# Encoder layer on one core: the second group's queries, keys and values as block products in a stage of their own

## The chip, the cores and the metric

The kernel runs on one core of a Trainium2 chip, in one launch. The metric is the device time of that core in microseconds, from the start of the program to its end. Lower is better. Each kernel is timed in several executions, and one more execution is recorded by the profiler.

## The reference

One layer (DEPTH is 1) over 2048 frames of width 1024, with 16 heads of 64 and an FFN of width 2816, all in fp32. Chunk c of 64 frames attends to itself and to the 8 chunks before it, with a learned relative bias for each head.

```
def rms_norm(x, g):
    return x * rsqrt(mean(x * x, axis=-1) + 1e-6) * g

# each chunk c of 64 frames, k0 = max(0, (c - 8) * 64), k1 = (c + 1) * 64
sc = einsum('bhqd,bhkd->bhqk', q[chunk c], k[:, :, k0:k1]) * 64 ** -0.5 + bias
o  = einsum('bhqk,bhkd->bhqd', softmax(sc), v[:, :, k0:k1])

h = rms_norm(x, g_pre_mix);  q, k, v = split_heads(h @ w_qkv)
x = x + rms_norm(merge_heads(o) @ w_o, g_post_mix)
h = rms_norm(x, g_pre_ffn)
x = x + rms_norm((silu(h @ w_gate) * (h @ w_up)) @ w_down, g_post_ffn)
```

## The kernel before

**Tiles.** The 2048 frames are two groups (NG) of 1024, each of two halves of 512 (HALF). Features lie on the 128 partitions, in eight blocks of 128 (KT), and frames run along the columns. An fp32 product is made of three matmuls over values that are split into a high and a low part: high by high, high by low, low by high (`products`, L187 to L191). Weights come from DRAM as raw tiles and are split on ScalarE and VectorE (`split_part`, L124).

**Stages.** First the attention of group 0 with its queries, keys and values, then that of group 1 with its own, then the FFN of both groups (`gate_up`, `down`). The FFN's products are already done by seven block products in place of eight (`Blocks`; the names B11, B21, T1, T2, B22, T3, T4 are the seven column sides, and `FACTOR` gives the weight block or sum of blocks of each). The weight sums S1 to S4 are made in DRAM by SyncE copies and by accumulating copies that GpSimd issues (`weight_sums`), one step at a time during the attention.

**Attention.** `Attend` is one half of one pair of heads: 16 jobs in a group, each of four query blocks of 128 frames. For one query block, TensorE makes the scores of both heads (tile `st`, L549 and L550), VectorE adds the bias and takes the maximum (L558), ScalarE takes the exponential and its sum (L562), VectorE the reciprocal (L565), GpSimd scales (L566). Then TensorE transposes (tile `tt`, L582 for four key blocks, L593 for the fifth), and ScalarE and VectorE copy the result to SBUF as `pT` (L585, L587, L594). The weighted sum of the values (`output`, tile `po`, L611) comes once in four query blocks, for the whole job.

**What fills in.** The dense products of queries, keys (`qk_job`), values (`v_job`) and of w_o (`o_half`) are a generator, `dense`, that yields after each product. `fill` takes products from it between the attention's parts, at the rate that the due times ask for; `until` takes them until a named result is there. Each product gives one credit to a list of small steps (`later`, `tick`): norms, loads, splits, each with a price. `drain` runs all that is left in the list at once. In group 0's `o_half` the small steps load and norm group 1's input (`Prep`) and end the first half (`Post.write`: y times its row scale times the gain, plus the residual, stored as `x1_d`). In the FFN the class `Late` does the like for y that was put into DRAM (`sums`, `rstd`, `write`; L1136 and L1139).

**Order.** TensorE's order is the order of the program, written out by hand (`manual_schedule` for PE). The order on the other engines and on SyncE's DMA queue is set by a scheduler. Results of `o_half` for group 0 stay in SBUF. `y`, `res` and the columns that are loaded share one ring of three buffers of 128x512 (tag `io`).

```
def tick(w):
    credit[0] += w
    while later and credit[0] >= later[0][0]:
        cost, step = later.popleft()
        credit[0] -= cost
        step()

def drain():
    while later:
        later.popleft()[1]()
```

## Time and profile before

| what | value |
|---|---|
| three timed runs | 2445.75, 2446.17, 2447.52 us (median 2446.17) |
| profiled execution | 2441.23 us |
| span of its trace | 2439.5 us |
| mean granted TensorE clock | 0.995 |
| TensorE busy (matmul) | 2400.2 us, 98% |
| VectorE, ScalarE, GpSimd busy | 60%, 42%, 12% |
| group 0's last weighted sum | ends near 485 us |
| group 1's attention | to about 1056 us |
| first FFN matmul | 1149 us |
| DMA | 488.41 MB, 200 GB/s on average |

The busy share is an average over the stages. Where TensorE is full, a stage is as long as its matmuls. What ended an idle stretch of an engine is named behind an arrow in the profile's rows (`<-`). An instruction's duration there is longer than its distance to the next one, since matmuls are pipelined: the price of a matmul is the distance of two starts.

### The profile page before, as it was taken

Reading aid. Unit: us, or ns where it says so; the run is one execution under the profiler, and the core shown is the slowest. Engines: PE = TensorE matmul, PEld = TensorE weight load, DVE = VectorE, ACT = ScalarE, POOL = GpSimd, SP = SyncE. Lnnn points to the kernel's source line nnn. Section 1 sums busy time; section 2 is a strip of 40 time slices with the busy share of each in tenths; the row PEclk is TensorE's granted clock in tenths of the full one; section 3 lists DMA queues with packets and bytes.
Section 4 is the critical chain, followed back from the end, with each engine's and each line's share of the span. In section 5 each row is a group of like instructions: output and inputs, shape, how many; then the busy total and the mean of one; then the engine's idle time right before and its main releaser. Section 6 shows DMA issues by size and latency. Waiting matters only on the chain.

```text
span 2439.5 us, 34920 instructions
## 1 busy us (share of the span) xinstructions
PE 2400.2 (98%) x12554; PEld 1994.3 (82%) x12554; DVE 1466.2 (60%) x2569; ACT 1033.1 (42%) x1807; POOL 299.2 (12%) x379
## 2 busy tenths in 40 slices
PE   9999999899999999999999999999999999999997
PEld 8887887688888888778888788888888888888886
DVE  6555454577455554567567665577566655555577
ACT  5444444554344443455333333365343333334444
POOL 0223333202232322310000000000000000000001
PEclk9999999999999999999999999999999999999999
DMA  7689999957777766646476755477667655457654
GB/s 223 179 213 245 257 263 230 271 185 211 197 192 189 181 157 144 163 146 229 152 260 206 244 174 167 123 247 256 208 211 250 219 178 160 136 169 243 196 187 147
DMA packets 209884, 488.41 MB, mean 200 GB/s; under 512 B 25360, under 2 KB 27424, under 8 KB 208432
## 3 DMA queue, kind: packets, MB, share of 16 engines
q1 hardware_dynamic: 197040, 451.59, 58.4%
q0 software_dynamic: 12672, 34.61, 9.2%
q8 instruction: 99, 1.62, 0.3%
q14 instruction: 73, 0.60, 0.1%
HBM read 356.54 MB, written 148.42 MB: 207 GB/s over the span
## 4 chain that ended last, share of the span: by engine, by line
PE 52%; DMA 2%; DVE 2%; issue 0%; ACT 0%; SPq 0%; DVEq 0%; ACTq 0%
PE pd L190 6%; PE pd L189 6%; PE pd L191 6%; PE pb L189 4%; PE pb L191 4%; PE pb L190 4%; PE pa L189 3%; PE pa L191 3%; PE pa L190 3%; PE pc L189 3%; PE pc L190 3%; PE pc L191 3%; PE mm L189 1%; PE mm L191 1%; PE mm L190 1%; DMA y<-y 1%
## 5 line engine op out<-in xcount | busy, mean ns | idle before, releaser
L562 ACT ACTIVATE sc<-sc,nmax 128x640 f32<-128x640 f32 (+4 forms) x256 | 193.3, 756 | 280.7 <-DVE nmax L558 279.8
L189 PE MATMUL mm<-hb,whi 128*128 128x512 f32 x704 | 290.7, 413 | 3.5 <-ACT y L236 3.5
L191 PE MATMUL mm<-hb,wlo 128*128 128x512 f32 x704 | 277.6, 394 | 0.0
L190 PE MATMUL mm<-hb,whi 128*128 128x512 f32 x704 | 276.5, 393 | 0.0
L566 POOL TENSOR_SCALAR sc<-sc,rows 128x640 f32<-128x640 f32 (+4 forms) x256 | 194.1, 783 | 512.1 <-DVE rows L565 498.8
L558 DVE CUSTOM_DVE_ANT_0 sc<-st,bias 128x640 f32<-128x640 f32 (+4 forms) x256 | 179.8, 738 | 103.5 <-PE st L550 100.8
L189 PE MATMUL pb<-hb,whi_gu_T 128*128 128x512 f32 x528 | 206.1, 390 | 3.5 <-DVE terms L969 3.5
L190 PE MATMUL pb<-hb,whi_gu_T 128*128 128x512 f32 x528 | 205.5, 389 | 0.0
L191 PE MATMUL pb<-hb,wlo_gu_T 128*128 128x512 f32 x528 | 205.4, 389 | 0.0
L259 POOL TENSOR_TENSOR rs<-ms,neg_half 128x4 f32<-128x4 f32 (+1 forms) x11 | 16.7, 1520 | 1246.8 <-DVE ms L257 1246.8
L189 PEld LDWEIGHTS mm<-hb,whi 128*128 128x128 f32 x704 | 133.1, 189 | 38.1 <-issue 14.7
L191 PEld LDWEIGHTS mm<-hb,wlo 128*128 128x128 f32 x704 | 132.7, 188 | 29.3
L190 PEld LDWEIGHTS mm<-hb,whi 128*128 128x128 f32 x704 | 133.5, 190 | 19.5
L190 PE MATMUL pd<-a,whi_d_T 128*128 128x512 f32 (+1 forms) x368 | 140.0, 380 | 0.4 <-DVE a L342 0.4
L189 PE MATMUL pd<-a,whi_d_T 128*128 128x512 f32 (+1 forms) x368 | 140.0, 381 | 0.0
L191 PE MATMUL pd<-a,wlo_d_T 128*128 128x512 f32 (+1 forms) x368 | 139.7, 380 | 0.0
L189 PE MATMUL pa<-hb,whi_gu_B 128*128 128x512 f32 x352 | 137.5, 391 | 0.5 <-ACT terms L950 0.5
L549 PE MATMUL st<-k,q 128*128 128x384 f32 (+1 forms) x448 | 132.7, 316 | 4.9 <-DVE nmax L558 3.0
L191 PE MATMUL pa<-hb,wlo_gu_B 128*128 128x512 f32 x352 | 137.0, 389 | 0.0
L190 PE MATMUL pa<-hb,whi_gu_B 128*128 128x512 f32 x352 | 137.0, 389 | 0.0
L189 PE MATMUL mm<-whi,hb 128*128 128x256 f32 x448 | 132.8, 296 | 0.0
L126 DVE TENSOR_TENSOR wlo_gu_T<-raw,whi_gu_T 128x1024 fp32r<-128x1024 f32 x88 | 107.5, 1221 | 42.1 <-ACT whi_gu_T L125 41.7
(219 smaller groups left out, 5640.3 us busy)
## 6 DMA issues: line engine op xcount, KB each, us to landing
raw<-gu_S SPq DMA_DIRECT2D x88, 512.0 KB, 3.9
raw<-in_w_gu SPq DMA_DIRECT2D x66, 512.0 KB, 4.0
q<-stage SPq DMA_DIRECT2D x128, 256.0 KB, 5.4
y<-y SPq DMA_DIRECT2D x96, 256.0 KB, 3.9
gu_S<-in_w_gu SPq DMA_DIRECT2D x44, 512.0 KB, 6.9
raw_a<-aT SPq DMA_DIRECT2D x88, 256.0 KB, 3.6
raw_d<-d_S SPq DMA_DIRECT2D x88, 256.0 KB, 3.5
raw<-in_w_a SPq DMA_DIRECT2D x42, 512.0 KB, 5.4
```

What stands on the lines that cost most here:

```text
L126: dve.tensor_tensor(lo, raw, hi.bitcast(F32), op=ALU.subtract)
L189: pe.matmul(pt, a_hi, b_hi, start=first, stop=False, skip_group_check=go_on)
L190: pe.matmul(pt, a_hi, b_lo, start=False, stop=False, skip_group_check=go_on)
L191: pe.matmul(pt, a_lo, b_hi, start=False, stop=last, skip_group_check=go_on)
L259: pool.tensor_tensor(r[0][:, :nb], m[:, :nb], neg_half.to_broadcast([P, nb]), op=ALU.pow)
L549: pe.matmul(st[:, a:b], q[:, 2 * h, cols], kk[:, h, key], start=True, stop=False)
L558: dve.tensor_tensor_reduce(out=sc[:, :n], in0=st[:, c0 : c0 + n], in1=rev, scale=-1.0, scalar=3.0e38, op0=ALU.add, op1=ALU.min, accum_out= ...
L562: act.activation(sc[:, :n], sc[:, :n], AF.Exp, bias=nmax, scale=-1.0, accum_out=rows[:, 0:1])
L566: last_pool[0] = pool.tensor_scalar(sc[:, :n], sc[:, :n], rows[:, 1:2], 1.0, op0=ALU.mult, op1=ALU.mult)
```

## The change

Group 1's queries, keys and values leave the attention. They are made between group 0's attention and group 1's, by seven block products for each block of four (`AttentionBlocks`, `qk_stage`, `v_stage`), and stored in DRAM (`qk_d`, `v_d`). Group 1's attention (`attend_second`) loads them back one pair of heads at a time. There the transposes follow the scores by two query blocks, and the weighted sum, now one query block at a time in pieces of 128 columns (`deep_output`), by three. Group 0's second half of w_o, which was done ahead of group 1's attention, now fills this attention, 0.8 us a block for as long as it lasts, and the products of group 1's own w_o its end.

Group 0's output of w_o goes to DRAM (`yo_d`), and `Late` ends both of its halves, with a new last part that also sums the squares of the result (`next`, one-column matmuls) and keeps the row scale for the FFN (`keep`). The weight sums get six more units of eight steps for the new blocks; 40 steps are done in the first attention.

```
+    yo_d = [dram.tile([P, KT, HALF], F32, name=f"yo_{i}") for i in range(2)]
...
+        def deep_output(self, ib):
+            for n, (r, b) in enumerate(self.blocks(ib)):
+                v = vs[g, s - 1 + (ib + b) // 4, j]
+                for h in range(2):
+                    pe.matmul(
+                        self.po[heads[h], cols], v[:, (ib + b) % 4, c : c + 64], self.pT[:, h, r, cols],
...
+    def qk_stage(b):
...
+        for c in range(NPAIR // 2):
...
+            pa = [bank("pa") for _ in range(2)]
+            yield from product(pa, "B11", True, copy(pa, p1))
+            yield from product(pa, "B21", False, lambda i: keep(pa[i], 0, 0, i))
+            pc = [bank("pc") for _ in range(2)]
+            yield from product(pc, "T1", True, copy(pc, p5))
+            if c == 0:
+                drain()
+            pb = [bank("pb") for _ in range(2)]
+            yield from product(pb, "T2", True, u)
+            yield from product(pc, "B22", False, closing(pc, u2, 1, 0, ALU.add))
+            yield from product(pb, "T3", False, closing(pb, p5, 1, 1))
+            yield from product(pb, "T4", False, closing(pb, p1, 0, 1))
...
     class Late:
...
                 sp.dma_start(self.dst[:, dt, :], y)
+                if self.keep is not None:
+                    if dt == 0:
+                        self.next = nrm_tile("next", 1)
+                    add_square(y, self.next, dt == 0)
+            steps = [(w, lambda dt=dt: one(dt)) for dt in range(KT)]
+            if self.keep is not None:
+                steps.append((3.0, lambda: rstd_steps(self.next, None, keep=self.keep)[0][1]()))
...
     def dense():
...
+        later.extend(own.spreads() + pause(1.0) + own.plain(2.0, "B11", "B21"))
+        yield from o_half(0, 0, own.combined(2.5), 4, last=True)
+        drain()
+        own.waiting()
+        late = Late(yo_d[0], POST_MIX, x[0], x1_d[0], blocks[0].r[0])
+        later.extend(own.plain(1.5, "B22") + [(0.0, lambda: later.extend(
+            pause(8.0) + late.sums(8.0) + late.rstd(40.0) + late.write(10.0)))])
+        yield from qk_stage(own)
+        yield from v_stage(own)
+        drain()
+        close_ffn()
+        open_attention()
+        yield from o_half(0, 1)
+        late1 = Late(yo_d[1], POST_MIX, x[1], x1_d[1], blocks[0].r[1])
+        later.extend(late1.sums(2.0) + late1.rstd(12.0) + late1.write(3.0))
+        yield from o_half(1, 0, blocks[0].spreads() + pause(1.0) + blocks[0].first(2.5), 4)
...
+    def attend_second():
...
+        fill(8.0)
+        for t in range(slots + 4):
+            rate = 3.0 if t < 2 else (0.8 if t < slots - 8 else 2.4)
+            if t < slots:
...
+                job.scores(ib)
+                if t % 3 != 2:
+                    next(sums, None)
+            fill(0.3 * rate)
+            for lag, do in ((2, "deep_transposed"), (3, "deep_output"), (2, "deep_fifth")):
+                if 0 <= t - lag < slots:
+                    getattr(jobs[(t - lag) // 4], do)((t - lag) % 4)
+                if lag == 3:
+                    fill(0.7 * rate)
+            tick(4.0)
```

How instructions stand in the two programs shows at three places. The first is TensorE in the middle of group 1's attention. Before, a query block has the scores (`st`), the transposes (`tt`) and a product's matmuls (`mm`) between them:

```order
L549 MATMUL st<-k_7_10375,q_0_7_10269 128x384
L550 MATMUL st<-k_7_10375,q_0_7_10269 128x384
L189 MATMUL mm<-hb_11_5766,whi_0_9718 128x512
L190 MATMUL mm<-hb_11_5766,whi_0_9718 128x512
L191 MATMUL mm<-hb_11_5766,wlo_0_9719 128x512
L582 MATMUL tt<-ident,sc 128x128 x8
L189 MATMUL mm<-hb_11_5766,whi_0_9718 128x512
L190 MATMUL mm<-hb_11_5766,whi_0_9718 128x512
L191 MATMUL mm<-hb_11_5766,wlo_0_9719 128x512
```

Now, in the blocks where `o_half(0, 1)` is used up, transposes, weighted sum (`po`) and the next scores stand directly behind each other:

```order
L548 MATMUL tt<-ident,sc 128x128 x8
L574 MATMUL po<-pT,v_0_2_9286 64x128 x4
L574 MATMUL po<-pT,v_-1_2_9284 64x128 x6
L560 MATMUL tt<-ident,sc 128x128 x2
L472 MATMUL st<-k_4_9104,q_1_4_9345 128x384
```

No product's matmul stands between the parts of these blocks any more.

The second place is TensorE in the first column of `qk_stage`, which is new. `pc` is the product T1, `pb` the product T2, and `total`, `rs` and `next` belong to `Late` of the first half:

```order
L185 MATMUL pc<-hb_9_5353,whi_qk_at_T_5551 128x512
L186 MATMUL pc<-hb_9_5353,wlo_qk_at_T_5552 128x512
L254 MATMUL pssq<-ones,total 128x1 [waits DVE_49]
L254 MATMUL pssq<-ones,total 128x1 x3
L270 MATMUL prs<-ident,rs 128x128 [waits Pool_49]
L270 MATMUL prs<-ident,rs 128x128 x3
L254 MATMUL pssq<-ones,next 128x1 [waits DVE_49,PE_49]
L254 MATMUL pssq<-ones,next 128x1 x3
L184 MATMUL pb<-hb_12_5535,whi_qk_at_T_5555 128x512
```

The three small groups of `Late` stand between the matmuls of T1 and those of T2.

The third place is VectorE at the same point. L1271 and L1274 are the two operations of a step of `Late.write`, L240 the addition of its squares, L961 the first use of T2:

```order
L256 TENSOR_SCALAR ms<-pssq 128x4 [waits PE_49]
L1271 SCALAR_TENSOR_TENSOR y<-y,gt,total 128x512 [waits DMAHW4_49,Activation_49]
L1271 SCALAR_TENSOR_TENSOR y<-y,gt,total 128x512 [waits DMAHW6_49,DVE_49]
L1274 TENSOR_TENSOR y<-res,y 128x512 [waits DMAHW5_49,DVE_49]
L1274 TENSOR_TENSOR y<-res,y 128x512 [waits DMAHW1_49,DVE_49]
L240 TENSOR_TENSOR next<-next,sq 128x512 [waits Activation_49]
...
L1274 TENSOR_TENSOR y<-res,y 128x512 [waits DMAHW3_49,DVE_49]
L240 TENSOR_TENSOR next<-next,sq 128x512 [waits Activation_49]
L256 TENSOR_SCALAR ms<-pssq 128x4 [waits PE_49]
L961 TENSOR_TENSOR terms<-terms,pb 128x512 [waits PE_49] x2
```

The whole of `Late`, eight steps with waits for their DMAs, stands ahead of VectorE's part of T2.

More of the change, by code (lines that the diff above doesn't have):

```diff
@@ L533, in scores @@
             ap = phase["ap"]
-            if (g, p, "bias") not in bias:
-                bias[g, p, "bias"] = [bias_tile(NH * g + 2 * p + h, 2 * p + h) for h in range(2)]
+            load_bias(g, p)
             q, kk = qs[g, s, p], ks[g, p]
@@ new lines, in dense @@
+        yield from begin()
+        said.add(("start", 0))
+        for p in range(1, NPAIR):
+            qw = take()
+            if p == 2:
+                later.extend(own.sums(8.0))
+            for s in range(2):
+                yield from qk_job(0, s, p, qw)
+                said.add(("qk", 0, s, p))
+            if p % 2 == 0:
+                vw = take()
+                for s in range(2):
+                    yield from v_job(0, s, p // 2, vw)
+        later.extend(own.spreads() + pause(1.0) + own.plain(2.0, "B11", "B21"))
@@ new lines, in dense @@
+        said.update([("start", 1)] + [("qk", 1, s, p) for s in range(2) for p in range(NPAIR)])
+        yield from o_half(0, 1)
+        late1 = Late(yo_d[1], POST_MIX, x[1], x1_d[1], blocks[0].r[1])
+        later.extend(late1.sums(2.0) + late1.rstd(12.0) + late1.write(3.0))
+        stream.extend(factor_stream(gate_up_at, c, n) for c in range(NC) for n in BLOCKS)
+        yield from o_half(1, 0, blocks[0].spreads() + pause(1.0) + blocks[0].first(2.5), 4)
+        drain()
+        yield from o_half(1, 1, blocks[0].plain(3.0, "B21", "B22"), 0, last=True)
@@ L1312, in dense @@
+        drain()
         for step in blocks[0].third(0.0):
@@ L1424, in until, with finish_heads, attend_first @@
             tick(c / (3 * C512))
-    for g in range(NG):
-        until(("start", g))
+    def finish_heads(g):
+        for s in range(2):
+            if (g, s) in ats or ("pv", g, s, NPAIR - 2) not in said or ("qk", g, s, NPAIR - 1) not in said:
+                continue
+            if g == 0 and s == 0 or g == 1 and ("o", 0, s) in said:
+                gather(g, s)
+    def attend_first():
+        g = 0
         spent[0] = owed[0] = 0.0
```

592 lines of the change are left out of this document (332 added, 260 removed).

## The prediction

> **What bounds the kernel now.** I read the page's busy shares first, then stretches of the span (columns: stretch, its length, busy us and count on PE, PEld, DVE, ACT and POOL, the granted PE clock, the DMA share, GB/s), because an average over stages hides which engine ends a stage.
>
> ```profile
> PE 2400.2 (98%) x12554; PEld 1994.3 (82%) x12554; DVE 1466.2 (60%) x2569; ACT 1033.1 (42%) x1807; POOL 299.2 (12%) x379
> ...
> 180.00:360.00 180.00, 179.97 (x1126) 149.84 (x1125) 100.06 (x254) 75.68 (x170) 55.61 (x75) 1.00 0.95 254
> 560.00:1010.00 450.00, 449.71 (x2933) 380.15 (x2932) 246.99 (x554) 188.45 (x372) 128.43 (x157) 1.00 0.70 176
> 485.00:1149.00 664.00, 659.49 (x3977) 548.16 (x3978) 396.37 (x799) 297.31 (x556) 150.40 (x182) 1.00 0.67 180
> 2100.00:2160.00 60.00, 60.00 (x266) 49.68 (x265) 29.02 (x35) 18.94 (x24) 0.00 (x0) 1.00 0.45 138
> ```
>
> TensorE is the bound: 98% busy, and of the 664 us that the change rewrites (from the last weighted sum of group 0 to the first FFN matmul, the 485:1149 row) only 4.5 us are idle. So what the change takes from PE is gained in full, and what makes PE wait is lost in full; no slack is left to hide a wait in. The 60 us row of the FFN gives the price of a dense 128x512 matmul: 60.00 / 266 = 0.2256 us. The profiled execution took 2441.23 us, 1.7 over its span; the median of the runs, 2446.17, is 4.9 above it. My sum is made on 2441.2, and 4.9 is added at the end.
>
> **The products removed and added.** These rows are group 1's attention before, where product matmuls stand between the attention's own (start, duration, engine, line, out<-in, form, count):
>
> ```profile
> 840.71 4.53 PE L611 MATMUL po<-pT,v 128*64 128x512 f32 x32
> 845.17 0.38 PE L189 MATMUL mm<-whi,hb 128*128 128x256 f32 x1
> ...
> 846.35 1.03 PE L582 MATMUL tt<-ident,sc 128*128 128x128 f32 x8
> 847.14 0.36 PE L189 MATMUL mm<-whi,hb 128*128 128x256 f32 x1
> 847.34 0.28 PE L190 MATMUL mm<-wlo,hb 128*128 128x256 f32 x1
> 847.46 0.28 PE L191 MATMUL mm<-whi,hb 128*128 128x256 f32 x1
> ...
> 849.02 0.38 PE L593 MATMUL tt<-ident,sc 128*128 128x128 f32 x2
> 849.16 0.36 PE L189 MATMUL mm<-whi,hb 128*128 128x256 f32 x1
> ...
> 849.59 0.34 PE L549 MATMUL st<-k,q 128*128 128x384 f32 x1
> ...
> 850.77 0.28 PE L189 MATMUL mm<-whi,hb 128*128 128x256 f32 x1
> ...
> 1053.37 0.39 PE L611 MATMUL po<-pT,vh 128*64 128x128 f32 x4
> 1053.59 0.81 PE L611 MATMUL po<-pT,v 128*64 128x384 f32 x4
> ```
>
> A 128x256 matmul starts 0.12 us after the one ahead (847.34 to 847.46). Group 1's queries and keys are 768 matmuls of 512 columns, its values 768 of 256: 768 x 0.2256 + 768 x 0.12 = 265.4 us go. Seven block products per block cost 336 of 512 columns for each of the three terms, 1008 x 0.2256 = 227.4 us. **A: -38.** As the stretch before is full, this is a gain as long as PE is fed.
>
> **The attention's own matmuls.** In the 450 us row stand (each product group three times, for its three terms):
>
> ```profile
> L189 PE MATMUL mm<-hb,whi 128*128 128x512 f32 x245 | 102.2, 417 | 0.0
> L189 PE MATMUL mm<-whi,hb 128*128 128x256 f32 x256 | 75.6, 295 | 0.0
> L582 PE MATMUL tt<-ident,sc 128*128 128x128 f32 x432 | 55.9, 272 | 0.0
> ```
>
> 736 products of 512 columns (166.0) and 768 of 256 (92.2) leave 191.5 us for 432 / 8 = 54 query blocks: 3.55 us each. Its pieces by the rows: scores 1.18 (849.59 to 850.77), eight transposes 0.79 (846.35 to 847.14), two more 0.14, a quarter of a weighted sum 4.46 / 4 = 1.11; together 3.22. The other 0.33 is the change from one kind of matmul to the next: the first product after transposes takes 0.20 (847.14 to 847.34) where the others take 0.12. The new order has about two such changes fewer in a block, so I take 3.4: 64 x 0.15 = 10 us, and the 4 us of idle time in the old stage go with it. **B: -14.** The new weighted sums run 128 columns at a time, and the 128-column rows here (four in 0.22 us, 0.055 each) give 20 x 0.055 = 1.10 a block, the same as now. But these four stand between longer ones, under which the weights are loaded. The transposes, an unbroken stream of 128-column matmuls with a new weight each, take 0.79 / 8 = 0.099; at that the 20 would take 1.98. I stay near the row of the same operation: **P: +4** (0 to +28, half way to the transposes). [...]
>
> **The block behind the third product.** In the new dense stage the flush after T1 of column 0 pops not only the columns of B22 but the whole step that ends group 0's first half: eight loads and squares, the row scale, eight steps of load, scale, add, store, square. In PE's order the one-column matmuls on `total` and on `next` stand between T1 and T2, and PE works in order: T2 waits until all eight steps are through. The same step exists before in the FFN, where it is spread out; SyncE's rows show its pace (DMA issues of the first two of eight steps and of the last, then a wait (total us, times, longest us), landing times and groups, the mean ns of one behind the busy time):
>
> ```profile
> 1231.90 0.32 SPq L68 DMA_DIRECT2D x<-y  x1
> 1232.28 0.42 SPq L68 DMA_DIRECT2D res<-in_x  x1
> ...
> 1236.06 0.32 SPq L68 DMA_DIRECT2D x<-y  x1
> ...
> 1273.81 0.32 SPq L68 DMA_DIRECT2D x<-y  x1
> ...
> DVE y L1136 <- DMA y<-y: 37.4, 20, 4.1
> y<-y SPq DMA_DIRECT2D x96, 256.0 KB, 3.9
> x<-y SPq DMA_DIRECT2D x32, 256.0 KB, 3.7
> res<-in_x SPq DMA_DIRECT2D x32, 256.0 KB, 4.7
> L259 POOL TENSOR_TENSOR rs<-ms,neg_half 128x4 f32<-128x4 f32 (+1 forms) x11 | 16.7, 1520 | 1246.8 <-DVE ms L257 1246.8
> L401 DVE SCALAR_TENSOR_TENSOR y<-y,gt,nrm 128x512 f32<-128x512 f32 x8 | 5.5, 744 | 2.7 <-ACT nrm L272 2.7
> L240 ACT ACTIVATE sq<-sum 128x512 f32<-128x512 f32 x14 | 8.8, 629 | 9.2 <-POOL sc L566 2.5 <-DMA sum<-x 2.3 <-issue 2.2
> L126 DVE TENSOR_TENSOR wlo<-raw,whi 128x1024 fp32r<-128x1024 f32 x24 | 30.1, 1255 | 10.9 <-ACT whi L125 10.9
> ```
>
> Eight stores from 1231.90 to 1273.81 are 5.99 us apart on average, 4.16 at the least. The ring of three buffers sets this: the next residual is loaded only once an add has freed its buffer, and needs about 4 us to land. The FFN also paces these steps by its products, so I take 5.0 for the flushed step. After T1's end: about half of DVE's 13 rows ahead (three weight splits of 1.255, four scales of 0.744, six subtractions of 0.69, 10.9 us against T1's own 24 x 0.2256 = 5.4), 5.5; eight sums through the ring, 8 x (3.9 + 0.63 + 0.69) / 3 = 14, of which some 3 lie under that, 11; row scale with the power on POOL (1.52), 3; first step 1.5, seven more 35; last square, add and sum 1.5. **D: +57.** Low end: DVE's own work without any wait, 5.5, then 8.1 (eight adds of 0.69, a split, two adds of the terms), 3, 8 x (0.744 + 2 x 0.69) and 1.3: 35. High end at 5.99 a step and all 14 us: 70. Nothing else on PE can run there, since its order is fixed. Behind it the clock:
>
> ```profile
> 466.22 0.80 PE L189 MATMUL mm<-hb,whi 128*128 128x512 f32 x1 [3.52 <-ACT y L236]
> 466.82 0.63 PE L190 MATMUL mm<-hb,whi 128*128 128x512 f32 x1
> 467.24 0.63 PE L191 MATMUL mm<-hb,wlo 128*128 128x512 f32 x1
> ```
>
> After 3.52 us idle the products are 0.42 apart instead of 0.2256, for about 3 us. **K: +2** (1 to 4).
>
> **Other waits.** T1's first factor: DVE has 51 rows between group 0's last weighted sum and the weights of T1 (three splits, 16 scales, 32 adds and subtractions: 37.7 us), PE has 96 + 48 matmuls, 32.5 us. With the first column's landing **C: +7** (2 to 15). The columns for it and group 0's attention cost other engines only: 0 there.
>
> Start of the second attention: the first keys come from DRAM behind the last stores of values in SyncE's queue, so a store (3.7 us, like x<-y) and six loads of keys and queries (about 8) follow the last product, 12.5 with its eviction; 8 us of output products are put ahead as cover. **E: +5** (1 to 12).
>
> In the attention, 22 of 64 blocks (33 to 51, 57 to 59) have no product beside them, and the same ending step of the second half runs through this stretch: its sum row stands about three blocks ahead of the row scale and seven (7 x 3.4 = 24 us) ahead of the last sum. Its eight steps need 41 us at 5.0, and DVE, working in order, holds the attention's reduces behind each wait for a residual. **F: +15** (0 to 35). The groups of the old stage show what one such block asks of DVE:
>
> ```profile
> L558 DVE CUSTOM_DVE_ANT_0 sc<-st,bias 128x640 f32<-128x640 f32 x110 | 86.4, 822 | 42.9 <-PE st L550 41.3 <-issue 1.2
> L558 DVE DVE_READ_ACCUMULATOR2_ANT nmax<- 128x1 f32 x110 | 9.1, 83 | 0.0
> L565 DVE RECIPROCAL rows<-rows 128x1 f32<-128x1 f32 x110 | 17.8, 162 | 25.9 <-ACT sc L562 25.1
> L585 DVE COPY pT<-tt 128x512 f32<-128x512 f32 x54 | 37.0, 685 | 15.7 <-PE tt L582 14.8
> L617 DVE COPY ot<-po 128x512 f32<-128x512 f32 x13 | 9.0, 692 | 30.3 <-PE po L611 30.3
> ```
>
> 2 x (0.822 + 0.083 + 0.162) + 0.685 + 0.692 / 4 = 2.99 us against PE's 3.4: a margin of 0.4 a block with four engines in a chain, where before a block's own products gave 3 or 4 us. **H: +8**, half of 22 x 0.7 (0 to 15).
>
> DMA: I count 89 MB in the second attention (keys, queries and values read back, heads, residuals, two weight-sum steps in three blocks). At the 254 GB/s that the 180:360 row moved with PE full they take 350 us, against 270 us of PE work there (64 x 3.4 and 234 products) and 33 of waits. That row's share is 0.95, and PE did not wait; half the accumulating copies can be late without anyone waiting. **G: +5** (0 to 43). The sums moved into group 0's attention and into the dense stage: no PE row there waits for them, 0. The FFN's order is unchanged: 0.
>
> **The sum.** -38 - 14 + 4 + 57 + 2 + 7 + 5 + 15 + 8 + 5 = +51: 2441.2 + 51 + 4.9 = 2497.
>
> **Rivals.** (1) Faster: transfers run ahead, and the flushed step takes DVE's work alone. Then D is 35, F, G, H and P are 0, C 2, E 1: -38 - 14 + 35 + 2 + 2 + 1 = -12, 2434. The measured 4.16 as smallest distance and 20 waits of DVE for y speak against it. It decides where C, D, E, F, G, H, K and P together stay below 52 us. Chance 0.14. (2) The second attention is bound by transfers: 350 us instead of 307, so another 43 in place of nothing in the sum, 2540. For it: the share of 0.95 already at 254 GB/s. Against it: not all of the 89 MB has a date. Chance 0.17. (3) The weighted sums are bound by weight loads: P +28 instead of 4, and H's 8 vanishes below it, 2513. The 0.055 row does not show it, though it is no unbroken stream. Chance 0.10. [...]
>
> **How the numbers follow.** My forecast, the sum of the terms, has 0.57 (its own range 2465 to 2530, D and F off by 20 each and not together); 0.02 is for what I don't see. A measurement of this kernel tells about 0.2%, 4.9 us, from no change. Rival 1 is faster nearly as a whole, with a little from the forecast's edge: 0.14 faster, 0.03 the same, 0.83 slower. The range leaves rival 1 out and takes in rival 2: 2450 to 2548.
>
> **What would show it.** In the changed profile: one PE idle stretch of 35 to 70 us behind T1 of column 0, released by DVE or POOL, in which DVE's rows wait for `res` and `y` (D); a slice of the page with PE near 1 or 2 tenths; PE rows of 64x128 at 0.055 to 0.08 (P); PE idle of 10 to 40 us in blocks 33 to 51, ended by DVE (F, H); DMA share near 1 there without PE waiting for keys (G). I am wrong if PE's idle time behind T1 is below 30 us, or if PE waits for keys and values in the second attention block after block.

## The result and the profile after

The changed kernel takes 2638.36 us (median of four executions, 2633.61 to 2643.79) against 2445.96 before: a ratio of 1.0794, with a 95% interval of 1.0763 to 1.0824. That is 192.4 us slower. The forecast was 51 slower, so the sign was right and the size was not.

The page's first lines (busy time of each engine, then the granted TensorE clock and the DMA share in 40 slices) show what changed in kind:

```profile
PE 2422.0 (92%) x12794; PEld 2011.7 (76%) x12794; DVE 1526.5 (58%) x2624; ACT 1091.7 (41%) x1913; POOL 321.0 (12%) x411
...
PEclk9999999967999989779989999999999999999999
DMA  7779889776899999895955675537757764456654
```

No other engine has become the bound: VectorE is at 58%. TensorE's busy time grew although it has less to do, because the clock was lower in the dense stage (slices 8 and 9, counted from 0), in the second attention (14, 16 and 17) and where the FFN begins (20). The stretches are group 0's part, the dense stage, the second attention, group 1's own w_o, and the FFN (columns as in the prediction):

```profile
0.00:495.40 495.40, 474.25 (x2913) 396.23 (x2913) 277.47 (x667) 229.01 (x491) 124.02 (x179) 0.98 0.81 218
495.40:845.00 349.60, 274.55 (x1200) 225.41 (x1200) 180.75 (x238) 112.45 (x159) 21.55 (x32) 0.89 0.85 254
845.00:1253.00 408.00, 325.04 (x2690) 276.32 (x2691) 210.83 (x519) 199.34 (x437) 142.94 (x176) 0.89 0.86 224
1253.00:1325.10 72.10, 68.96 (x306) 55.92 (x304) 48.95 (x67) 27.68 (x41) 8.89 (x11) 1.00 0.95 277
1325.10:2641.80 1316.70, 1279.23 (x5688) 1057.86 (x5688) 808.53 (x1135) 523.19 (x788) 23.59 (x14) 0.99 0.61 195
```

A stretch less its PE time is idle: 75.1 us in the dense stage, 83.0 in the second attention, 37.5 in the FFN. The PE time I split once more: in pieces of 2 us, busy time times the share of the clock that was not granted is time lost to the clock, and the rest is matmul work at full clock. Both profiled executions, whole spans, in us:

| | idle | lost to the clock | work at full clock | sum |
|---|---|---|---|---|
| before | 39.4 | 6.3 | 2393.8 | 2439.5 |
| after | 219.7 | 45.2 | 2376.9 | 2641.8 |
| difference | +180.3 | +38.9 | -16.9 | +202.3 |
| forecast | +93 | +2 | -44 | +51 |

The single waits of PE in the changed kernel (total us, times, longest):

```profile
PE pssq L254 <- DVE next L240: 37.2, 1, 37.2
PE st L472 <- DVE nmax L481: 29.2, 7, 11.3
PE pssq L254 <- DVE total L240: 24.0, 4, 13.3
PE tt L548 <- POOL sc L489: 21.4, 8, 4.6
PE pa L184 <- ACT terms L958: 18.8, 1, 18.8
PE po L574 <- DVE ot L585: 11.9, 1, 11.9
PE pa L184 <- ACT terms L1085: 11.6, 2, 10.3
...
PE st L472 <- DMA bias<-ext_d: 10.2, 1, 10.2
```

The first, with half of the third, is the predicted block behind T1. It shows in PE's rows, and VectorE's rows in it show the pace of the ending step (in brackets the idle time ahead and what ended it):

```profile
546.81 0.79 PE L184 MATMUL pa<-hb,whi_qk_at_B 128*128 128x512 f32 x1 [18.82 <-ACT terms L958]
...
572.78 1.87 PE L254 MATMUL pssq<-ones,total 128*128 128x1 f32 x8 [13.29 <-DVE total L240]
576.02 1.12 PE L270 MATMUL prs<-ident,rs 128*128 128x128 f32 x4 [1.37 <-POOL rs L258]
...
614.35 1.84 PE L254 MATMUL pssq<-ones,next 128*128 128x1 f32 x8 [37.22 <-DVE next L240]
```

```profile
586.18 0.69 DVE L1274 TENSOR_TENSOR y<-res,y 128x512 f32<-128x512 f32 x1 [6.36 <-DMA res<-in_x]
...
612.12 0.69 DVE L1274 TENSOR_TENSOR y<-res,y 128x512 f32<-128x512 f32 x1 [1.80 <-DMA res<-in_x]
```

13.29 + 1.37 + 37.22 = 51.9 us of idle time, and the second to the last step's additions, six apart, start from 586.18 to 612.12, 4.32 us each. The granted clock while PE stood there and just behind, and at the second attention's longest weighted-sum wait and behind it, is the first number after POOL's count:

```profile
559.50:614.35 54.85, 2.98 (x12) 2.53 (x13) 22.76 (x34) 10.75 (x17) 2.75 (x3) 0.54 0.72 211
614.35:618.00 3.65, 3.65 (x13) 3.26 (x14) 0.16 (x1) 0.00 (x0) 1.03 (x1) 0.50 0.46 146
1061.00:1073.00 12.00, 0.14 (x3) 0.11 (x4) 5.68 (x7) 3.40 (x7) 4.27 (x6) 0.54 0.94 261
1073.00:1077.00 4.00, 2.91 (x22) 2.17 (x22) 0.69 (x1) 1.01 (x2) 0.54 (x1) 0.50 0.74 155
```

Behind such a wait PE works some 3 to 7 us at half clock (granted 0.50): about 3 us from 546.81 on, about 7 from 614.35 on. One such wait was in the forecast, at +2; the changed kernel has them in the dense stage, in the FFN and most of all in the second attention, and over the whole span 38.9 us more were lost to the clock than before. How long a wait has to be for this, the two traces don't settle: behind one of 2.83 us (to 1181.94) the granted clock was 0.50 for some 6 us, and in the kernel before, behind one of 3.40 us (to 457.51), it was 1.00 for the next 5 us.

### The profile page after: what moved, and what is told of

Read it like the earlier page. It is cut to its first block, busy times and chain, and to the rows that moved or that the text cites. A ratio compares the mean times of both kernels' runs of the same rounds, so it can differ in the third digit from the quotient of the medians.

```text
span 2641.8 us, 36015 instructions
## 1 busy us (share of the span) xinstructions
PE 2422.0 (92%) x12794; PEld 2011.7 (76%) x12794; DVE 1526.5 (58%) x2624; ACT 1091.7 (41%) x1913; POOL 321.0 (12%) x411
## 2 busy tenths in 40 slices
DMA packets 247266, 564.51 MB, mean 214 GB/s; under 512 B 27920, under 2 KB 38176, under 8 KB 246832
## 4 chain that ended last, share of the span: by engine, by line
PE 71%; DMA 14%; DVE 6%; issue 4%; ACT 2%; SPq 1%; POOL 1%; DVEq 0%; POOLq 0%; ACTq 0%
PE pd L185 6%; PE pd L186 6%; PE pd L184 6%; PE pb L184 5%; PE pb L185 5%; PE pb L186 5%; PE pa L184 3%; PE pa L186 3%; PE pa L185 3%; PE pc L184 3%; PE pc L186 3%; PE pc L185 3%; PE mm L184 3%; PE mm L185 3%; PE mm L186 3%
## 5 line engine op out<-in xcount | busy, mean ns | idle before, releaser
L184 PE MATMUL pb<-hb,whi_gate_up_at_T 128*128 128x512 f32 x528 | 207.1, 392 | 7.3 <-DVE terms L1104 7.3
L185 PE MATMUL pb<-hb,whi_gate_up_at_T 128*128 128x512 f32 x528 | 206.2, 390 | 0.0
L186 PE MATMUL pb<-hb,wlo_gate_up_at_T 128*128 128x512 f32 x528 | 206.0, 390 | 0.0
L184 PE MATMUL mm<-hb,whi 128*128 128x512 f32 x448 | 186.7, 417 | 0.0
L472 PE MATMUL st<-k,q 128*128 128x384 f32 (+1 forms) x448 | 140.3, 332 | 41.1 <-DVE nmax L481 29.2
L186 PE MATMUL mm<-hb,wlo 128*128 128x512 f32 x448 | 176.4, 394 | 1.6 <-DVE wlo L131 1.6
L185 PE MATMUL mm<-hb,whi 128*128 128x512 f32 x448 | 176.3, 394 | 0.0
L184 PE MATMUL pa<-hb,whi_gate_up_at_B 128*128 128x512 f32 x352 | 139.6, 397 | 12.4 <-ACT terms L1085 11.6
L186 PE MATMUL pa<-hb,wlo_gate_up_at_B 128*128 128x512 f32 x352 | 138.9, 395 | 3.9 <-DVE wlo_gate_up_at_B L131 3.9
L184 PE MATMUL pd<-a,whi_d_T 128*128 128x512 f32 (+1 forms) x368 | 140.0, 380 | 0.0
L185 PE MATMUL pa<-hb,whi_gate_up_at_B 128*128 128x512 f32 x352 | 138.7, 394 | 0.0
L473 PE MATMUL st<-k,q 128*128 128x384 f32 (+1 forms) x448 | 134.4, 319 | 0.0
L131 DVE TENSOR_TENSOR wlo_gate_up_at_T<-raw,whi_gate_up_at_T 128x1024 fp32r<-128x1024 f32 x88 | 107.5, 1221 | 41.2 <-ACT whi_gate_up_at_T L130 40.9
L130 ACT ACTIVATE whi_gate_up_at_T<-raw 128x1024 fp32r<-128x1024 f32 x88 | 93.1, 1058 | 91.3 <-PE pa L185 35.2
L184 PEld LDWEIGHTS pb<-hb,whi_gate_up_at_T 128*128 128x128 f32 x528 | 99.5, 189 | 29.9 <-DVE terms L1104 9.4
```

The lines of the kernel that those rows point to most:

```text
L130: act.activation(hi, raw, AF.Copy)
L131: dve.tensor_tensor(lo, raw, hi.bitcast(F32), op=ALU.subtract)
L184: pe.matmul(pt, a_hi, b_hi, start=first, stop=False, skip_group_check=go_on)
L185: pe.matmul(pt, a_hi, b_lo, start=False, stop=False, skip_group_check=go_on)
L186: pe.matmul(pt, a_lo, b_hi, start=False, stop=last, skip_group_check=go_on)
L472: pe.matmul(st[:, a:b], q[:, 2 * h, cols], kk[:, h, key], start=True, stop=False)
```

## The experiments

Each experiment was timed beside the kernel before, whose median was 2445.77 to 2451.10 us. "Above before" is the difference of the two medians; the changed kernel stands at +192.4. The intervals of the ratios are about 0.3% to each side, so two kernels less than some 10 us apart aren't told apart. Diffs are against the changed kernel. Three kernels leave work out: e2 and e11 the accumulating copies of the weight sums from the second attention on, e5 and e11 the ending step of group 0's second half, whose place a copy of its input takes.

**The flush behind T1.** e1_spread lets the ending step of the first half run at its own pace beside the products:

```
 yield from product(pc, "T1", True, copy(pc, p5))
-if c == 0:
-    drain()
 pb = [bank("pb") for _ in range(2)]
```

> The flush after T1 of column 0 is left out, so that the step that ends group 0's first half is spread over the dense stage by its credits. Theory (the flushed step stops TensorE because TensorE's order is fixed): the idle 13.3 + 1.4 + 37.2 us between T1 and T2 and some 4 us of halved clock behind it go, 2638 - 56 = 2582. Rival (VectorE and the transfers are the bound of the dense stage, and the step costs the same wherever it stands): the waits come back later in the stage, 2620 to 2640.

2598.98 us, ratio 1.0629 [1.0605, 1.0654]: +153.2, so 39 less. The waits for `next` and behind T1 are gone, but four new ones came ahead of products on `pb`, of 1.18 to 3.61 us, the longest this:

```profile
581.20 0.50 PE L184 MATMUL pb<-hb,whi_qk_at_T 128*128 128x512 f32 x1 [3.61 <-DVE terms L966]
```

They make 11.6 us together. So the flush costs about 52 us of idle time, of which the spread steps cost 11.6 again: VectorE stands in their waits, and the next product's terms stand behind it.

**The weight sums beside the second attention.** e2_noadd leaves out the accumulating copies that GpSimd issues there:

```
-            yield [f(to, a) for f, to, a in step]
+            yield [f(to, a) for f, to, a in step if f is copy or "deep" not in phase]
```

> In the second attention and behind it the weight sums keep their plain copies, but the accumulating copies that GpSimd issues are left out (the FFN's weight sums are then incomplete). Theory (GpSimd's scaling of the scores stands behind accumulating copies in GpSimd's own queue, which wait for the busy DMA): TensorE's waits for `sc`, 21.4 us in 8 places, and the halved clock behind each of them go, -30, 2608. Rival (the DMA load itself makes the attention late, or VectorE does): the waits stay or move to another engine, at most -10, 2628. Beyond 2600 also the start of the FFN would be shown to be late because of these copies.

2599.87, ratio 1.0628 [1.0600, 1.0657]: +154.1, 38 less. All of the waits `tt L548 <- POOL sc` are gone; the span's idle time fell from 219.7 us to 184.8 and the time lost to the clock from 45.2 to 36.5. GpSimd's rows in the changed kernel show how such a wait arises, and its stretch shows the DMA share (1.05):

```profile
879.93 0.85 POOL L862 DMA_DIRECT2D gu_S<-gu_S  x1 [7.80 <-issue]
880.53 1.85 POOL L489 TENSOR_SCALAR sc<-sc,rows 128x640 f32<-128x640 f32 x2
889.48 0.85 POOL L862 DMA_DIRECT2D gu_S<-gu_S  x1 [7.09 <-issue]
890.08 3.38 POOL L489 TENSOR_SCALAR sc<-sc,rows 128x640 f32<-128x640 f32 x4
...
891.23 1.92 PE L548 MATMUL tt<-ident,sc 128*128 128x128 f32 x8 [3.91 <-POOL sc L489]
...
880.00:890.00 10.00, 5.54 (x44) 4.30 (x44) 4.06 (x12) 2.60 (x6) 2.91 (x4) 1.00 1.05 298
```

Ahead of the row of one accumulating copy GpSimd stands for 7.09 us and waits for nothing that the profile shows. The edit takes the copies' traffic away as well (564.51 MB became 549.83), so it doesn't part the queue from the load on the DMA; for the queue speaks that the waits that went are those for GpSimd, while those of the scores for VectorE stayed (29.2 us before, 30.5 after). Behind the copy stand the scalings of the scores, two query blocks at once (four in 3.38 us), and the transposes behind those. The kernel before had the same at the same copies, unseen in the prediction:

```profile
321.36 0.85 POOL L857 DMA_DIRECT2D gu_S<-gu_S  x1 [5.55 <-issue]
...
364.42 0.87 POOL L857 DMA_DIRECT2D gu_S<-gu_S  x1 [7.32 <-issue]
```

There products stood beside every block, and PE's transposes waited 0.7 us for GpSimd in the whole span, in spite of the 5.55 and 7.32 us.

e6_sums does the steps in the attention every fourth block instead of two in three, and the rest one to a product of the FFN's first `gate_up`:

```
+            if g == 0:
+                next(sums, None)
...
-                if t % 3 != 2:
+                if t % 4 == 0:
                     next(sums, None)
...
-    for _ in sums:
-        pass
```

> Nothing is left out. The weight sums that the second attention need not have ready, those for the FFN's second product, are issued in the FFN's first stage instead, one step a product; the attention keeps 16 steps of 43, and none is left behind it. Theory (GpSimd's queue): as where the accumulating copies were left out, 2600, and the start of the FFN earlier by up to 10 besides, since no copies stand at the attention's end: 2590 to 2600. Rival (they cost the FFN what they cost the attention): 2625 to 2640.

2621.04, ratio 1.0698 [1.0676, 1.0721]: +169.9, 22 less. The attention's waits for GpSimd are gone, and the FFN got new ones, the longest this:

```profile
1374.95 0.47 PE L270 MATMUL prs<-ident,rs 128*128 128x128 f32 x1 [8.14 <-POOL rs L258]
```

The row scale's power is also GpSimd's. So two kinds of small work that share this queue with the copies were held up: the scalings (PE waited 21.4 us for them in the changed kernel) and the row scale (8.14 us here).

**The ending step in the attention.** Four kernels ask what about it costs. e3_late1 gives it more room (the products of group 0's second half are used up faster, 1.6 us a block instead of 0.8, so that they end earlier, and the steps are dearer, so that they spread over more blocks):

```
-        later.extend(late1.sums(2.0) + late1.rstd(12.0) + late1.write(3.0))
+        later.extend(late1.sums(4.0) + late1.rstd(12.0) + late1.write(10.0))
...
-            rate = 3.0 if t < 2 else (0.8 if t < slots - 8 else 2.4)
+            rate = 3.0 if t < 2 else (1.6 if t < 20 else (0.8 if t < slots - 8 else 2.4))
```

> The products of group 0's second half are used up at 1.6 us a block instead of 0.8, so that they end at block 17 or so, and the ending step of that half is spread over blocks 20 to 55 instead of 33 to 47. Theory (VectorE holds the attention's reduces behind the waits of that step's transfers): the long waits of TensorE there (11.9, 7.8, 9.9, 11.3 and smaller ones, 46 us) and the halved clock behind them (some 15 us) go for the most part, -45, 2593. Rival (the blocks without products are bound by DMA or by GpSimd): the time goes into other waits, 2615 to 2640, since there are now 14 more such blocks.

2637.82, ratio 1.0786 [1.0766, 1.0807]: +192.1, no difference. Spread out, the step costs what it cost before. In SyncE's rows of this kernel a store stands ahead of the next load, and VectorE waits for the load while the attention's maximum stands behind it:

```profile
1042.32 0.32 SPq L70 DMA_DIRECT2D x<-y  x1
...
1045.34 0.55 SPq L70 DMA_DIRECT2D y<-yo  x1
...
1052.17 0.75 DVE L1271 SCALAR_TENSOR_TENSOR y<-y,gt,total 128x512 f32<-128x512 f32 x1 [6.04 <-DMA y<-yo]
...
1056.36 0.69 PE L472 MATMUL st<-k,q 128*128 128x384 f32 x1 [9.35 <-DVE nmax L481]
```

A store is not the only thing that holds a load up. The longest wait of the second attention in the changed kernel, 11.9 us for `ot`, lies in the step's sums, where the step has not stored anything yet. There the load of `y` stands in SyncE's queue behind the attention's own loads, of which the four of the biases take 8.84 us (rows of the changed kernel):

```profile
1051.28 8.84 SPq L70 DMA_DIRECT2D bias<-ext_d  x4
...
1061.61 0.33 SPq L70 DMA_DIRECT2D y<-yo  x1
```

e4_res gives the residual of the flushed first half's step buffers of its own, since the prediction held the ring of three for the cause of the pace:

```
-                y, res = io("y"), io("res")
+                y, res = io("y"), (narrow("res") if self.keep is not None and "fp" in phase else io("res"))
```

> The residual of the flushed step takes a buffer of another ring, so that its load need not wait for the add before it. Theory (the ring of three buffers sets the pace of 4.6 us a step, by the residual's landing): the idle of 37.2 us falls to VectorE's own work, some 22, so -15, 2623. Rival (the pace is the transfers' own throughput or VectorE's work): 37 us as before, 2638.

2634.76, ratio 1.0775 [1.0755, 1.0794]: +189.0, within the error of no difference. With a free buffer the residual's load still leaves right behind the store of the step before:

```profile
588.74 0.32 SPq L70 DMA_DIRECT2D x<-y  x1
589.11 0.42 SPq L70 DMA_DIRECT2D res<-in_x  x1
```

The store waits for the add (from 588.02; an add takes 0.69 us in the rows above, so until 588.71), and the load behind it in SyncE's queue leaves 0.37 us after the store. The additions are still 4.2 us apart (588.02 to 605.00 in four steps). The residual's buffer was not the cause; `y` kept the ring of three.

e5_nolate1 leaves the second half's ending step out:

```
-        later.extend(late1.sums(2.0) + late1.rstd(12.0) + late1.write(3.0))
+        sp.dma_start(x1_d[1], x[1])
+        dve.tensor_copy(blocks[0].r[1], blocks[0].r[0])
```

> The ending step of group 0's second half (row scale, residual, sum of squares) is left out of the second attention: its result is only a DRAM copy of the input, and the row scale of the other half is used. Theory (this step's transfers on VectorE's and SyncE's queues cost the attention its long waits): the waits of 9 to 12 us between 1060 and 1160 us and the halved clock behind them go, 2638 - 60 = 2578. Rival (the blocks without products are slow by themselves, by DMA or GpSimd): 2610 or more.

2607.71, ratio 1.0644 [1.0624, 1.0665]: +156.6, 36 less. That is what the step costs in all where it stands. Its waits of the scores for VectorE went:

```profile
PE tt L548 <- POOL sc L489: 30.2, 15, 6.3
...
PE st L472 <- DVE nmax L481: 7.6, 5, 2.9
```

29.2 us became 7.6, while 21.4 us behind GpSimd became 30.2: the two causes stand beside each other and hide one another in part.

e7_whole does the whole step, but all 16 loads ahead of it, into two tiles that are free in this stage, so that no load stands behind a store:

```
...
+        def loads(self, w):
+            self.yt, self.rt = (hb_tile(n, F32, (KT, HALF)) for n in (2, 3))
...
-        late1 = Late(yo_d[1], POST_MIX, x[1], x1_d[1], blocks[0].r[1])
-        later.extend(late1.sums(2.0) + late1.rstd(12.0) + late1.write(3.0))
+        late1 = Whole(yo_d[1], POST_MIX, x[1], x1_d[1], blocks[0].r[1])
+        later.extend(late1.loads(0.5) + pause(6.0) + late1.sums(2.0) + late1.rstd(8.0) + late1.write(4.0))
```

> Nothing is left out. The ending step of the second half loads all of y and of the residual ahead, into two tiles that are free by then, so that no VectorE instruction waits for a transfer that SyncE issues behind a store of the same step. Theory (the queue of SyncE closes a ring: store waits for add, next load stands behind the store, add waits for load, and the attention's reduces stand behind the add): nearly all that leaving the step out gains, but for its 24 us of VectorE's own work, 2638 - 45 = 2593. Rival (the step costs VectorE time, not waits): 2620 to 2640.

2612.67, ratio 1.0659 [1.0636, 1.0683]: +161.6, 31 of the 36 back. The waits of the scores for VectorE fell from 29.2 us to 10.8, and the one for `ot` is gone. So the step's arithmetic costs little, and nearly the whole cost is the wait for loads that come late. The edit takes these loads out of the ring of three too, and buffers alone were tried only in the dense stage (e4). That SyncE's queue and not the ring makes them late is, for this copy of the step, read from the rows and not shown by a run.

**The FFN.** TensorE's and the code's order there is as before, but its idle time doubled. ScalarE's rows at its beginning:

```profile
1338.32 0.63 ACT L239 ACTIVATE y<-y 128x512 f32<-128x512 f32 x1 [4.46 <-DMA y<-y]
...
1346.67 0.62 ACT L239 ACTIVATE y<-y 128x512 f32<-128x512 f32 x1
1347.19 0.58 ACT L1085 ACTIVATE terms<-pa 128x512 f32<-128x512 f32 x1
...
1347.82 0.80 PE L184 MATMUL pa<-hb,whi_gate_up_at_B 128*128 128x512 f32 x1 [10.33 <-ACT terms L1085]
```

Squares that wait for loads now stand ahead of the copy that frees PE's bank. `Late.sums` squares in place in the changed kernel, where it used a scratch tile before, and the scheduler then puts the squares earlier on ScalarE. e9_sq undoes this line alone:

```
-                add_square(c, self.total, dt == 0, sq=c)
+                add_square(c, self.total, dt == 0)
```

> One word of the change is undone: in Late.sums the squares go into a tile of the scratch ring again, not over the loaded y. Theory (the squares of the FFN's first ending step, no longer held back by that ring, stand in ScalarE's order ahead of the first product's copy and wait there for their loads): the wait of 10.3 us at the start of the FFN, the one of 3.9 us ahead of it and the halved clock behind them go, 2638 - 17 = 2621. Rival (the start of the FFN is late because of the columns and weights, whose loads share the DMA with the left-over weight sums): 2633 to 2640.

2626.35, ratio 1.0736 [1.0702, 1.0769]: +179.1, 13 less, at the edge of what the intervals tell apart. The trace decides: `pa L184 <- ACT terms L1085` fell from 11.6 us to 2.6, and the FFN's stretch, from its first product to the end, from 1316.7 us to 1303.4, with 26.6 us of idle time for 37.5. Single waits of the attention changed places (those of the scores for VectorE rose from 29.2 us to 49.0, the one for `ot` went), but outside the FFN the time changed little (1320.5 us for 1325.1).

**One query block at a time.** e12_shallow keeps the dense stage and gives the second attention the old order (transposes one block behind the scores, the weighted sum once in four blocks):

```
...
-            for lag, do in ((2, "deep_transposed"), (3, "deep_output"), (2, "deep_fifth")):
...
+            if t > 0 and t % 4 == 0:
+                jobs[t // 4 - 1].output()
+            if t >= 0:
+                jobs[t // 4].transposed(t % 4, lambda: fill(0.7 * rate))
...
```

> Only the order inside the second attention is undone: transposes one block behind the scores and the weighted sum once in four blocks, as in the first attention, everything else as changed. Theory (with few products between, TensorE would wait for the chain from scores to scaled weights in every block): slower than the changed kernel, by 1 us in the filled blocks and 2 in the 22 unfilled ones, 2638 + 80 = 2718. Rival (the deeper order, with 128-column sums, is itself what costs the attention its time): faster than 2638 by 10 to 30.

2633.71, ratio 1.0768 [1.0734, 1.0803]: +186.4, no worse. I expected 80 more; the deeper order is worth nothing that can be measured in this kernel. Its idle time is the same (220.8 against 219.7), and its matmul work is 8.6 us less (2368.3).

**T1's factor, and the start of the attention.** e13_cols moves the splits of the T2 and T4 columns behind T1, to bring T1 forward (one of its three places is shown):

```
...
             yield from product(pc, "T1", True, copy(pc, p5))
             if c == 0:
+                b.waiting()
                 drain()
...
```

> The splits of the columns for T2 and T4 (8 of VectorE's 51 rows ahead of T1, 5.5 us, and 8 of ScalarE's) stand behind T1 instead of ahead of it. Theory (the amount of column work sets the wait ahead of the second product): the wait of 18.8 us falls to 12 to 14, and the wait behind T1 grows by as much, since the same queue runs on there: the same time, 2633 to 2639. Rival (one late load sets it): 18 to 19 us as before.

2639.42, ratio 1.0767 [1.0742, 1.0793]: +190.7, no difference. The wait behind T1 for `total` is gone, but the one ahead of the second product is longer by as much:

```profile
556.69 0.80 PE L184 MATMUL pa<-hb,whi_qk_at_B 128*128 128x512 f32 x1 [32.53 <-ACT terms L959]
```

The sum is 73.9 us against 70.7. VectorE's and ScalarE's work from group 0's end to T2 is the same and only stands elsewhere.

e14_fill puts 20 us of output products, not 8, ahead of the second attention (`fill(8.0)` becomes `fill(20.0)`):

> 20 us of w_o products stand ahead of the second attention instead of 8. Theory (the loads need some 18 us behind the last store of values, and 8 are covered): the wait of 10.2 us goes; as the same products are missing later, where blocks without products wait for VectorE and GpSimd more, 2630 to 2638. Rival (the products' own weights or the columns hold the start): the wait stays.

2640.18, ratio 1.0766 [1.0737, 1.0795]: +191.5. The wait of 10.2 us ahead of the first scores is gone, but the idle time of the span is the same, 220.0 us for 219.7, in later waits of up to 13.2 us: the 12 us of products were taken from blocks that then stood bare.

**Together.** e8_combo joins e1, e6, e7 and `fill(14.0)`; e10_best joins e1, e7, e9, `fill(14.0)` and the sums spread thinly over the dense stage, the attention (every third block) and the FFN (every second product); e15_all adds e13 and `fill(20.0)` to that; e11_off joins e1, e2, e5 and e9.

> Nothing is left out: the first half's step spread, the sums moved, the second half's step from whole tiles, and 14 us instead of 8 us of products ahead of the second attention. If the causes are separate, their gains add: -39 - 42 - 45 - 6 = -132, 2506. If they share the halved clock and the same slack, less: 2520 to 2560. Below 2446 only if the waits that stay (columns of the dense stage 19 us, start of the attention, start of the FFN) went as well.

> Nothing is left out: as the kernel with the spread step, the whole tiles and the longer start, with the squares in the scratch ring, and with the weight sums of the FFN's second product divided, 12 steps in the dense stage, 22 in the attention, the rest at every second product of the FFN from its second column on. Theory (the causes are separate): 96 us above the kernel before, less 17 for the squares and some 10 for GpSimd's queue in the FFN, so 70 above it. Rival (the FFN's start and its waits for GpSimd have another cause): 90 to 100 above it.

> Nothing is left out: the version with the spread step, whole tiles, divided weight sums and squares in the scratch ring, and in addition both of the edits above. Theory (separate causes): 70 above the kernel before, less 5 for the columns and 6 for the start: 60 above it, and still slower than before, since the waits that stay at the stage changes and the half clock behind them (some 90 us) are more than the 38 us of matmuls that the seven products save. A version faster than before would have to lose 60 us more.

> All the causes found so far are taken away together, for accounting: the first half's step spread, the second half's step left out (a DRAM copy of the input in its place), no accumulating copies in and behind the second attention, squares in the scratch ring. If the causes are separate and I have the large ones, 194 - 40 - 37 - 40 - 17 = 60 above the kernel before; what stays are the columns ahead of the dense stage (19 us), the start of the attention (10), the end of group 0's attention (10) and the attention's own matmuls. If they hide behind one another, 90 or more above.

| kernel | us | ratio | above before |
|---|---|---|---|
| e8_combo | 2547.39 | 1.0395 [1.0376, 1.0415] | +96.3 |
| e10_best | 2517.73 | 1.0289 [1.0253, 1.0324] | +70.4 |
| e15_all | 2522.41 | 1.0296 [1.0264, 1.0327] | +73.7 |
| e11_off | 2499.30 | 1.0217 [1.0178, 1.0256] | +52.0 |

In e11_off the four causes are away: their single gains, 39 + 38 + 36 + 13 = 126, came to 140. They account for most of the 192. The flush was in the forecast at about its size; the other three are what it lacked or sized wrongly. In the profiled execution of e11_off, 103.2 us of idle time, 22.8 lost to the clock and 2370.3 of work remain: 23.5 us less work than before (the left-out step's few small matmuls are part of it) is bought with 63.8 more idle time and 16.5 of clock. The kernels that do all the work get back up to 122 us (e10_best). In e10_best waits such as this one remain, with VectorE's terms late:

```profile
1450.67 0.79 PE L184 MATMUL pb<-hb,whi_gate_up_at_T 128*128 128x512 f32 x1 [9.78 <-DVE terms L1107]
```

None of the versions run beats the kernel before.

## Why the prediction was wrong, term by term

The sign came from the right reading: PE had 4.5 us idle where the change was made, so a wait was lost in full, and what the products gained was small against it. The forecast of 2497 is 141 us short of the median. Against the table, 151 us of the profiled execution are missing: 87 idle, 37 clock, 27 work. Three steps failed: the waits of the second attention were put at 28 us (F, G, H) and are 73, the clock was charged behind one wait only (K), and the FFN was put at nothing. The work saved (A, B, P) was put 27 us too high.

**D, right:** +57 forecast, 51.9 measured, at the predicted place and at 4.32 us a step where 5.0 was taken. The size came from the pace of the same step in the FFN, so it held although the stated reason did not: buffers of its own for the residual left the pace as it was (e4), and the rows show the residual's load behind the store in SyncE's queue. (D's high end, given as 70, adds up to 67 by its own terms.)

**F, H and G, the largest miss:** 28 forecast for the waits of the second attention, and 83.0 - 10.2 = 73 measured (+45); 24.5 of the 45.2 us lost to the clock lie there too. F was +15, and e5 makes the step's whole price 36 us: its loads come late (e7), and the attention's work stands behind them on VectorE. What H alone costs was not parted from F and G. G was argued for the wrong victim: it asked whether transfers are late, and "half the accumulating copies can be late without anyone waiting" is true of their data. What waits is the scaling behind a copy in GpSimd's queue: leaving the copies out gave 38 us (e2). The row of 321.36 could have told it; the prediction read GpSimd's busy share, 12%, in which this standing time is not counted.

**K, wrong:** the clock was +2, for one long wait, and is +38.9. Behind all of the changed kernel's waits of 2.5 us and more the granted clock is 0.50 to 0.66 for the next 2.5 us. The clock was not tried by itself: less was lost to it where there was less idle time, 36.5 us beside 184.8 in e2 and 22.8 beside 103.2 in e11_off.

**"The FFN's order is unchanged: 0", wrong:** idle time rose by 18.8 us there. The code's order was unchanged and the scheduler's was not; one in-place square is 10.8 of it, and some 13 with its clock (e9). The rest is not settled.

**C and E, too small:** 18.8 against 7, and 10.2 against 5. C was reckoned for DVE's 37.7 us of work against 32.5 us of PE work. The wait came one product earlier than T1, ahead of B21, at the copy of B11's result in ScalarE's queue, which stands there behind column splits:

```profile
544.35 0.63 ACT L274 ACTIVATE hb<-sums 128x512 fp32r<-128x512 f32 x1 [0.57 <-DVE sums L817]
546.16 1.08 ACT L958 ACTIVATE terms<-pa 128x512 f32<-128x512 f32 x2 [1.18 <-DVE hb L275]
```

E's 8 us for six loads was the author's estimate: from the first key's load (836.92) to the first scores (850.82) it was 13.9 us, and the loads of the biases, which E did not count, ended the wait. Neither wait is removed by moving work (e13, e14): the idle time only changed its place.

**A, B and P:** together -48 was forecast (4 of it idle time) and the work fell by 16.9. Of the 27 us missing, 23 lie in the three rewritten stretches (637.2 us of work for 658.1 before). A block without products shows where:

```profile
1046.55 1.03 PE L548 MATMUL tt<-ident,sc 128*128 128x128 f32 x8
1047.51 0.66 PE L574 MATMUL po<-pT,v 128*64 128x128 f32 x8
1048.00 0.82 PE L574 MATMUL po<-pT,v_-1_2_9284 128*64 128x128 f32 x12
1048.76 0.44 PE L560 MATMUL tt<-ident,sc 128*128 128x128 f32 x2
1048.95 0.42 PE L472 MATMUL st<-k,q 128*128 128x384 f32 x1
...
1050.21 0.38 PE L548 MATMUL tt<-ident,sc 128*128 128x128 f32 x2
```

1046.55 to 1050.21 is 3.66 us where B took 3.40: 64 blocks at 0.26 more are 17 us. The transposes take 0.96 to the next operation, not 0.79, and each block still has four changes of kind. The 20 weighted sums take 1.25 us, 0.0625 each: 64 x (1.25 - 1.11) = 9 for P instead of 4. These 9 are part of the 17, and 4 were in the forecast, so the block explains 13 of the 23; the other 10 are not settled. e12, with the old weighted sum, has 8.6 us less work.

**The rivals.** Rival 1 (transfers run ahead) fell with D's measured pace. Rival 2 had its resource right, a DMA share up to 1.05, but PE did not wait for keys and values block after block; the busy DMA came with GpSimd standing long ahead of its copies instead. That the share makes them long is not shown: before, there were 5.55 and 7.32 us too. Rival 3 (weight loads) did not come: P is 9, not 28. Group 0's part, with 4.9 us more idle time and 2.1 of clock, was not tried.

## What to carry to other kernels

Small work that was hidden under big matmuls had a price that only showed when the matmuls left (PE waited 0.7 us for GpSimd's scalings before, 21.4 after): before moving products out of a stage, list for each queue (DMA issues on GpSimd, stores and late loads ahead of loads on SyncE, VectorE's waits for loads) what each item blocks, and for how long the remaining work covers it. A load whose data is needed soon should not be queued behind a store that waits for arithmetic, nor behind loads that are held up: loading all first gave back 31 of 36 us in the attention, where more room gave nothing; more buffers, tried in the dense stage, gave nothing there. And where a change makes many waits on TensorE such as these, of 2.5 us and more, count the clock behind each: here 39 us beside 180 us of idle time.

## What the runs showed of the hardware

Ahead of an accumulating copy GpSimd's queue often stood for 3 to 9 us (8.95 us at 925.01 of the changed kernel is the longest in the second attention), in which GpSimd counts as idle; a busy share of 12% said nothing about it. Squaring in place instead of through a scratch tile left the cost of a square as it was (629 ns, and 626 in e9) and moved ScalarE's order enough for about 13 us. And the deeper order of the second attention was worth nothing that could be measured (e12). A lead of one or two blocks more, 3.66 us each, against waits of 4 to 11 us may be too short to matter; longer leads were not tried.
